# Two heads at a time in a recurrence, weights by halves, and a hold on small products in a planned three-layer kernel

## The chip, the cores and the metric

The kernel runs on one core of a Trainium2 chip. The metric is the device time of one execution in microseconds. Its engines are TensorE (PE, its weight loads PEld), VectorE (DVE), ScalarE (ACT), GpSimd (POOL) and SyncE (SP), whose queue issues the DMAs.

## What is computed

Input `x` is 256 tokens of width 2048. Three layers follow, each with a projection in, a mixer, a projection out and a residual. The first layer joins a sparse attention (8 heads) with an RWKV recurrence (16 heads of 64); the second is a differential attention (A), the third a gated linear attention with 4 heads (B). What matters here, cut to the core:

```python
def compress(kv, pos, w1, w2):                      # first layer, keys and values in blocks of 32
    flat = blocks_of_32(kv + pos)                   # (15 blocks, 2 groups, 32 * 128)
    return silu(flat @ w1) @ w2                     # w1: 4096 x 128

def step(state, inp):                               # RWKV, 16 heads, 256 steps
    r_t, w_t, k_t, v_t, a_t, b_t = inp
    sa = einsum('bhij,bhj->bhi', state, a_t)
    state = state * w_t[:, :, None, :] + sa[..., None] * b_t[:, :, None, :] + v_t[..., None] * k_t[:, :, None, :]
    return state, einsum('bhij,bhj->bhi', state, r_t)

def step(state, xs):                                # layer B, 4 heads, 4 chunks of 64 tokens
    qi, ki, vi, ti = xs
    state = exp(ti)[..., None] * state + einsum('bchk,bchv->bhkv', ki, vi)
    return state, einsum('bchk,bhkv->bchv', qi, state)
```

## The kernel before

**Who makes the order.** The program's instructions are first recorded as `Op`s. `Plan.schedule` (L279) then gives each engine a fixed order: it keeps a heap of ready operations for each engine and takes the one that can start first by estimated costs and due times, with program order as the tie break. `Plan.run` (L377) adds `SWITCH` (170 ns) to an estimate when TensorE goes from one tile size to another; `part` (L120) is that size in quarters of rows and columns, (4, 4) being the whole array. Operations on TensorE are due `MARGIN` (700 ns) later than their data, or 1500 ns behind a DMA. Since all instructions are issued on one line, every row of the profile says L277, and one goes by tile names. A tile can start only when its tag has a buffer, in program order within the tag.

**The bulk.** `gemm` streams 2048x512 weight groups: ScalarE makes the high part `wh_*`, VectorE the low part `wl_*`, and TensorE runs three products for each (`acc_*`, fp32r, 256 to 512 columns). All else is put between these products.

**The recurrence.** `rwkv_group` (L795) treats four heads at a time (g = 0 to 3), tokens in four chunks c of 64. `pA` holds products of a chunk with itself, which VectorE masks into `AB`. GpSimd inverts a triangular block of it (`blocks`), and the result comes back by way of DRAM as `M1` and `X`; `pT`, `pY` and `pX` complete the inverse, `pV` makes `M2` (the profile drops the numbers: both are `M`). Then comes the loop over c (from L976): `pU` = M1 times M2, copied into `AVt`; `pS`, the state for the next chunk, into `M2`; and `yp`, the output, from `AB` and, behind the first chunk, from `RT` and `M2`. Every product is for one head: 64 columns, and the output on the half of the array that belongs to the chunk (c even or odd). `yp` is one PSUM tile for the whole loop; two PSUM buffers serve this stream. `bn_stats` (L1007) then reads `yp`.

**Compression.** `compress` (L1137) is a generator, advanced after each weight tile of the third group's `rk` and `v`. For keys, then values, it loads `w1` in four parts of 512 KB and multiplies 8 slices of each into `ph`, 32 rows of the output at a time.

**Layer B's scores.** `gla_scores` (L1570) makes, for each head, decayed keys `d` (profile: `kd`), `q1`, `q2` (`q`) and `k2` (`k`), whose second half GpSimd copies (L1596). For each half j of the key dimension, six products of 64x64 go into `pB` and then one whole-array product of `k2` and `q2`.

## Time and profile before

| | us |
|---|---|
| median of 3 runs | 1483.45 (1483.18 to 1488.77) |
| the profiled execution | 1483.21 |
| its span, first to last instruction | 1481.4 |
| TensorE busy | 1454.8 (98%) |
| VectorE busy | 967.3 (65%) |
| ScalarE busy | 768.4 (52%) |
| GpSimd busy | 316.4 (21%) |

A product in fp32 stands in the trace as two MATMUL records, one in fp32r as one. TensorE overlaps its records, so a record's own duration is longer than the distance to the next start; distances between starts are what to read. The view "order of time" merges neighbours of one kind and gives the start of the first, the time to the end of the last, and how many.

### The profile page before, as it was taken

Reading aid. Unit: us, or ns where it says so; the run is one execution under the profiler, and the core shown is the slowest. Engines: PE = TensorE matmul, PEld = TensorE weight load, DVE = VectorE, ACT = ScalarE, POOL = GpSimd, SP = SyncE. Lnnn points to the kernel's source line nnn. Section 1 sums busy time; section 2 is a strip of 40 time slices with the busy share of each in tenths; the row PEclk is TensorE's granted clock in tenths of the full one; section 3 lists DMA queues with packets and bytes.
Section 4 is the critical chain, followed back from the end, with each engine's and each line's share of the span. In section 5 each row is a group of like instructions: output and inputs, shape, how many; then the busy total and the mean of one; then the engine's idle time right before and its main releaser. Section 6 shows DMA issues by size and latency. Waiting matters only on the chain.

```text
span 1481.4 us, 24543 instructions
## 1 busy us (share of the span) xinstructions
PE 1454.8 (98%) x9437; PEld 1278.9 (86%) x9437; DVE 967.3 (65%) x1678; ACT 768.4 (52%) x1269; POOL 316.4 (21%) x402
## 2 busy tenths in 40 slices
PE   8999999999999999999999999999999998999998
PEld 8988889989999988788888888788888897988887
DVE  5876575575857754876767676656765567565554
ACT  6542345344545544757575757554544473455532
POOL 0258846615600000030404050100100001000000
PEclk9999999999999999999999999999999999999999
DMA  9545434636524567665556566556665553655564
GB/s 334 182 131 198 160 97 139 194 104 183 156 82 148 165 218 228 212 190 174 182 171 185 167 180 215 174 186 197 205 208 186 173 172 110 222 174 185 185 213 128
DMA packets 91957, 263.42 MB, mean 178 GB/s; under 512 B 19960, under 2 KB 26512, under 8 KB 91840
## 3 DMA queue, kind: packets, MB, share of 16 engines
q1 hardware_dynamic: 91840, 261.86, 56.6%
q8 instruction: 74, 1.21, 0.3%
q14 instruction: 43, 0.35, 0.1%
HBM read 253.92 MB, written 7.90 MB: 177 GB/s over the span
## 4 chain that ended last, share of the span: by engine, by line
PE 90%; DVE 6%; issue 1%; ACT 1%; DMA 1%; POOL 1%; SPq 0%; DVEq 0%; ACTq 0%
PE acc_Bo L277 6%; PE acc_Aq L277 6%; PE acc_Ao L277 6%; PE acc_o L277 6%; PE acc_Ak L277 6%; PE acc_Av L277 6%; PE acc_rk L277 6%; PE acc_Bg L277 6%; PE acc_Ag L277 5%; PE acc_Bv L277 5%; PE acc_zb L277 3%; PE acc_Bq L277 3%; PE acc_q L277 3%; PE acc_Bk L277 3%; PE acc_v L277 3%; PE acc_za L277 2%
## 5 line engine op out<-in xcount | busy, mean ns | idle before, releaser
L277 PE MATMUL acc_rk<-xp,wh_rk 128*128 128x256 f32 x512 | 96.7, 289 | 1.3 <-ACT wh_rk L277 1.3
L277 PE MATMUL acc_Bo<-mBp,wh_Bo 128*128 128x512 f32 x256 | 89.7, 396 | 0.0
L277 POOL TENSOR_TENSOR bt<-blocks 32x30 f32<-32x30 f32 (+14 forms) x120 | 87.5, 729 | 9.0
L277 PE MATMUL acc_Ao<-mAp,wh_Ao 128*128 128x512 f32 x256 | 89.3, 395 | 0.0
L277 PE MATMUL acc_Bv<-wh_Bv,xBp 128*128 128x412 f32 (+1 forms) x320 | 88.3, 355 | 0.0
L277 PE MATMUL acc_Aq<-wh_Aq,xAp 128*128 128x512 f32 x256 | 86.0, 407 | 0.7 <-ACT xAp L277 0.7
L277 PEld LDWEIGHTS acc_rk<-xp,wh_rk 128*128 128x128 f32 x512 | 80.6, 193 | 4.9 <-issue 2.6
L277 POOL TENSOR_TENSOR blocks<-blocks,bt 32x30 f32<-32x30 f32 (+14 forms) x120 | 80.8, 673 | 9.3
L277 PE MATMUL acc_Ag<-wh_Ag,xAp 128*128 128x512 f32 x256 | 81.6, 395 | 0.0
L277 PE MATMUL acc_Ak<-wh_Ak,xAp 128*128 128x512 f32 x256 | 80.8, 392 | 0.0
L277 PE MATMUL acc_Av<-wh_Av,xAp 128*128 128x512 f32 x256 | 80.8, 392 | 0.0
L277 PE MATMUL acc_Bg<-wh_Bg,xBp 128*128 128x512 f32 x256 | 80.5, 393 | 0.0
L277 PE MATMUL acc_o<-wh_o,mp 128*128 128x512 f32 x256 | 79.8, 392 | 0.0
L277 PE MATMUL acc_rk<-xp,wl_rk 128*128 128x256 f32 x256 | 72.9, 286 | 0.5 <-DVE wl_rk L277 0.5
L277 PE MATMUL acc_Bo<-mBp,wl_Bo 128*128 128x256 f32 x256 | 71.1, 280 | 0.0
L277 PE MATMUL acc_Ao<-mAp,wl_Ao 128*128 128x256 f32 x256 | 70.9, 279 | 0.0
L277 DVE TENSOR_TENSOR wl_o<-wr_o,wh_o 128x1024 fp32r<-128x1024 f32 x32 | 39.2, 1225 | 38.2 <-ACT wh_o L277 38.0
L277 DVE TENSOR_TENSOR wl_Bo<-wr_Bo,wh_Bo 128x1024 fp32r<-128x1024 f32 x32 | 39.2, 1224 | 36.0 <-ACT wh_Bo L277 36.0
L277 DVE TENSOR_TENSOR wl_Bg<-wr_Bg,wh_Bg 128x1024 fp32r<-128x1024 f32 x32 | 39.2, 1225 | 33.9 <-ACT wh_Bg L277 33.9
L277 ACT ACTIVATE wh_Bo<-wr_Bo 128x1024 fp32r<-128x1024 f32 x32 | 34.0, 1062 | 51.8 <-PE acc_Bo L277 48.5
L277 PEld LDWEIGHTS acc_Bv<-wh_Bv,xBp 128*128 128x128 f32 x320 | 60.1, 190 | 0.9
L277 DVE TENSOR_TENSOR wl_rk<-wr_rk,wh_rk 128x1024 fp32r<-128x1024 f32 (+1 forms) x33 | 41.5, 1260 | 29.0 <-ACT wh_rk L277 29.0
(731 smaller groups left out, 4426.4 us busy)
## 6 DMA issues: line engine op xcount, KB each, us to landing
wr_o<-w SPq DMA_DIRECT2D x32, 512.0 KB, 3.6
wr_Aq<-w SPq DMA_DIRECT2D x32, 512.0 KB, 3.7
wr_Ak<-w SPq DMA_DIRECT2D x32, 512.0 KB, 3.7
wr_Av<-w SPq DMA_DIRECT2D x32, 512.0 KB, 3.9
wr_Ag<-w SPq DMA_DIRECT2D x32, 512.0 KB, 3.6
wr_Ao<-w SPq DMA_DIRECT2D x32, 512.0 KB, 3.8
wr_Bg<-w SPq DMA_DIRECT2D x32, 512.0 KB, 4.3
wr_Bo<-w SPq DMA_DIRECT2D x32, 512.0 KB, 3.9
```

The source lines that it names most:

```text
L277: op.issued = getattr(getattr(self.nc, op.eng), op.method)(*op.args, **op.kw)
```

## The change

The loop of the recurrence takes two heads in one product: the stationary and the moving operand each hold two heads side by side, the output is 128x128, and only the two diagonal 64x64 blocks are read. For that the layouts of `AB`, `M1` and `X` are turned (chunks outside, heads inside), `RT` is a full-height tile with zeros where it holds nothing (a 1-buffer tag of its own), `M2` has a zeroed half for the first chunk, and `yp` is one PSUM tile for each chunk, copied by ScalarE into an SBUF tile `ys`, which replaces `y`. VectorE masks `pA` in two instructions instead of one, and adds the state in two.

`compress` loads `w1` in two halves of two DMAs into a tag with one buffer, and multiplies the 16 slices of a half in reverse order. In `gla_scores` VectorE copies `k2` in place of GpSimd, and the whole-array products come behind all twelve small ones of the head. The planner adds `HOLD`: a product on a part of the array enters the heap 800 ns after its data are due, but while the last product was on a part of the array, held ones that are due may be taken at once. `pc4` has 3 buffers in place of 4, and the DMA scratch is 512 in place of 1024.

```diff
@@ Plan @@
+    HOLD = 800
@@ schedule @@
+        held = set()
+        partial = lambda op: op.eng == "tensor" and op.part[:2] != (4, 4)
+
+        def push(op):
+            time = ready[op]
+            if partial(op):
+                held.add(op)
+                time += self.HOLD
+            heapq.heappush(later[op.eng], (time, op.key, op))
+
         def candidate(eng):
             free, ahead, behind = self.free[eng], now[eng], later[eng]
+            if eng == "tensor" and self.part and self.part[:2] != (4, 4):
+                near = [op for op in held if ready[op] <= free]
+                near = [op for op in near for time, tag in [buffer_time(op)] if tag is None and time <= free]
+                if near:
+                    op = min(near, key=lambda op: op.key)
+                    return free, op.key, op
...
@@ Kernel @@
-    BUFS = {"t1": 6, "t2": 10, "t4": 5, "tiny": 24, "rtiny": 12, "rt4": 4, "rt2": 2, "rt1": 2, "rt8": 1}
+    BUFS = {"t1": 6, "t2": 10, "t4": 5, "tiny": 24, "rtiny": 12, "rt4": 4, "rt4z": 1, "rt1": 2, "rt8": 1}
@@ rwkv_group @@
-        RT = self.sb(f"RT{g}", [128, 2, 4, 64], "rt2")
-        for i in range(2):
-            for o in range(2):
-                S.activation(RT[hf(o), :, i:4:2, :].rearrange("p c j t -> p j c t"), AV[hf(i), :, 1 - o:4:2, 2, :], AF.Copy)
+        RT = self.sb(f"RT{g}", [128, 4, 4, 64], "rt4z")
+        for o in range(2):
+            G.memset(RT[hf(1 - o), 1 - o:4:2], 0.0)
+            for i in range(2):
+                S.activation(RT[hf(o), 1 - o:4:2, i:4:2, :].rearrange("p c j t -> p j c t"), AV[hf(i), :, 1 - o:4:2, 2, :], AF.Copy)
...
-        AB = (self.work if g % 2 else self.big).tile([128, 4, 4, 2, 64], F32, name=f"AB{g}", tag="ml")
+        at = lambda c: c % 2 * 2 + c // 2
+        of = lambda c1: slice(2 * c1, 2 * c1 + 2)
+        AB = (self.work if g % 2 else self.big).tile([128, 2, 4, 4, 64], F32, name=f"AB{g}", tag="ml")
...
             for i in range(2):
-                V.tensor_tensor(AB[:, 2 * j + i].rearrange("p c k t -> p c (k t)"), ps[i],
-                                cst[:, None, C_SI:C_SI + 128].to_broadcast([128, 4, 128]), op=OP.mult)
+                for k in range(2):
+                    V.tensor_tensor(AB[:, k, :, 2 * j + i], ps[i][:, :, 64 * k:64 * k + 64],
+                                    cst[:, None, C_SI + 64 * k:C_SI + 64 * k + 64].to_broadcast([128, 4, 64]), op=OP.mult)
...
+        G.memset(M2[hf(1), 0], 0.0)
...
-        yp = self.ps(f"yp{g}", U3)
+        ys = self.sb(f"ys{g}", U3, "t2")
+        pair = lambda x, j: x[:, 2 * j:2 * j + 2].rearrange("p h x -> p (h x)")
+        own2 = lambda p: [(i, p[hf(i), :, hf(i)]) for i in range(2)]
         for c in range(4):
             c1, c2 = c % 2, c // 2
             own, oth = hf(c1), hf(1 - c1)
-            rows = slice(0, 128) if c else own
-            pu = self.ps(f"pU{g}{c}", (128, 4, 64))
-            for h in range(4):
-                mm(pu[own, h], M1[rows, h, c], M2[rows, c, h], start=(h == 0), stop=True, skip_group_check=True)
-            S.activation(AVt[own, c], pu[own], AF.Copy)
+            pu = self.ps(f"pU{g}{c}", (128, 2, 128))
+            for j in range(2):
+                mm(pu[:, j], pair(M1[:, at(c)], j), pair(M2[:, c], j), start=(j == 0), stop=True, skip_group_check=True)
+            for i, p in own2(pu):
+                S.activation(AVt[own, c, i:4:2], p, AF.Copy)
             if c < 3:
-                pS = self.ps(f"pS{g}{c}", (128, 4, 64))
-                for h in range(4):
-                    mm(pS[own, h], BKt[:, c, h], AVt[:, c, h], start=(h == 0), stop=True, skip_group_check=True)
-                pc = PC[own, c].rearrange("p j i -> p (j i)")[:, :, None].to_broadcast([64, 4, 64])
+                pS = self.ps(f"pS{g}{c}", (128, 2, 128))
+                for j in range(2):
+                    mm(pS[:, j], pair(BKt[:, c], j), pair(AVt[:, c], j), start=(j == 0), stop=True, skip_group_check=True)
                 Sn = M2[own, c + 1]
...
-            for h in range(4):
-                o = yp[own, c2 * 4 + h]
-                mm(o, AB[:, h, c, 1], AVt[:, c, h], start=(c2 == 0 and h == 0), stop=not c, skip_group_check=True)
+            yp = self.ps(f"yp{g}{c}", (128, 2, 128))
+            for j in range(2):
+                mm(yp[:, j], pair(AB[:, 1, at(c)], j), pair(AVt[:, c], j), start=(j == 0), stop=not c, skip_group_check=True)
             if c:
-                for h in range(4):
-                    mm(yp[own, c2 * 4 + h], RT[oth, c2, h], M2[oth, c, h], start=False, stop=True, skip_group_check=True)
+                for j in range(2):
+                    mm(yp[:, j], pair(RT[:, c], j), pair(M2[:, c], j), start=False, stop=True, skip_group_check=True)
+            for i, p in own2(yp):
+                S.activation(ys[own, 4 * c2 + i:4 * c2 + 4:2], p, AF.Copy)
...
-            V.bn_stats(st[:, u], yp[:, u])
+            V.bn_stats(st[:, u], ys[:, u])
@@ compress @@
-            for part in range(4):
-                w1 = self.sb(f"w1_{kind}{part}", [128, 8, 128], "t4")
-                nc.sync.dma_start(w1, a["cw1"][kind, part])
-                for l in range(8):
-                    ll, o = part * 8 + l, l % 4 * 32
-                    mm(ph[o:o + 32], wins[kind][:, ll], w1[:, l], start=(ll < 4), stop=(ll >= 28), skip_group_check=True)
-                if part < 3:
+            for half in range(2):
+                w1 = self.sb(f"w1_{kind}{half}", [128, 2, 8, 128], "w1")
+                for part in range(2):
+                    nc.sync.dma_start(w1[:, part], a["cw1"][kind, 2 * half + part])
+
+                for l in reversed(range(16)):
+                    ll, o = half * 16 + l, l % 4 * 32
+                    mm(ph[o:o + 32], wins[kind][:, ll], w1[:, l // 8, l % 8], start=(half == 0 and l >= 12), stop=(half == 1 and l < 4), skip_group_check=True)
+                if half == 0:
                     yield
@@ nsa_group @@
-        pc4 = [self.sb(f"pc{g}{t}", [128, 4, 4, 32], "pc4", bufs=4) for t in range(2)]
+        pc4 = [self.sb(f"pc{g}{t}", [128, 4, 4, 32], "pc4", bufs=3) for t in range(2)]
@@ gla_scores @@
-            G.tensor_copy(k2[:, :, 1], d[:, :, 1])
+            V.tensor_copy(k2[:, :, 1], d[:, :, 1])

             p = self.ps(f"pB{h}", (128, 3, 128))
+            st = lambda j: dict(stop=(j == 1), skip_group_check=True)
             for j in range(2):
-                st = dict(stop=(j == 1), skip_group_check=True)
                 for i, c in enumerate((0, 2)):
-                    mm(p[0:64, 2 * i, 0:64], d[:, j, c], q[:, j, c], start=(i == 0 and j == 0), **st)
-                    mm(p[0:64, 2 * i, 64:128], d[:, j, c], q1[:, j, i], start=False, **st)
-                    mm(p[64:128, 2 * i, 64:128], d[:, j, c + 1], q[:, j, c + 1], start=(i == 0 and j == 0), **st)
+                    mm(p[0:64, 2 * i, 0:64], d[:, j, c], q[:, j, c], start=(i == 0 and j == 0), **st(j))
+                    mm(p[64:128, 2 * i, 64:128], d[:, j, c + 1], q[:, j, c + 1], start=(i == 0 and j == 0), **st(j))
+                    mm(p[0:64, 2 * i, 64:128], d[:, j, c], q1[:, j, i], start=False, **st(j))
+            for j in range(2):
                 f2 = lambda x: x[:, j].rearrange("p c t -> p (c t)")
-                mm(p[:, 1], f2(k2), f2(q2), start=False, **st)
+                mm(p[:, 1], f2(k2), f2(q2), start=False, **st(j))
@@ kernel @@
-    nc = bacc.Bacc("TRN2", target_bir_lowering=False, num_devices=1, dynamic_dma_scratch_size=1024)
+    nc = bacc.Bacc("TRN2", target_bir_lowering=False, num_devices=1, dynamic_dma_scratch_size=512)
```

## Rows read from the trace of the kernel before

**Rows 1.** The page: span, and each engine's busy us (share) and instructions.

```profile
span 1481.4 us, 24543 instructions
...
PE 1454.8 (98%) x9437; PEld 1278.9 (86%) x9437; DVE 967.3 (65%) x1678; ACT 768.4 (52%) x1269; POOL 316.4 (21%) x402
```

**Rows 2.** Order of time, TensorE: start us, us, operation, records; group 0's loop.

```profile
164.56 0.28 PE L277 MATMUL acc_rk<-xp,wl_rk 128*128 128x256 f32 x1
164.77 0.68 PE L277 MATMUL pS<-AVt,BKt 128*64 128x64 f32 x8
165.29 0.63 PE L277 MATMUL yp<-AVt,AB 128*64 128x64 f32 x8
165.85 0.50 PE L277 MATMUL acc_rk<-xp,wh_rk 128*128 128x256 f32 x2
166.19 0.28 PE L277 MATMUL acc_rk<-xp,wl_rk 128*128 128x256 f32 x1
166.31 0.40 PE L277 MATMUL acc_rk<-xp,wh_rk 128*128 128x256 f32 x2
...
166.66 0.40 PE L277 MATMUL acc_rk<-xp,wh_rk 128*128 128x256 f32 x2
166.99 0.68 PE L277 MATMUL pU<-M,M 128*64 128x64 f32 x8
167.60 0.39 PE L277 MATMUL acc_rk<-xp,wl_rk 128*128 128x256 f32 x1
167.82 0.40 PE L277 MATMUL acc_rk<-xp,wh_rk 128*128 128x256 f32 x2
```

**Rows 3.** Order of time, TensorE: the last visit of group 3's loop.

```profile
430.07 0.68 PE L277 MATMUL yp<-AVt,AB 128*64 128x64 f32 x8
430.68 0.67 PE L277 MATMUL yp<-M,RT 64*64 64x64 f32 x8
431.28 0.39 PE L277 MATMUL acc_q<-xp,wh_q 128*128 128x256 f32 x1
```

**Rows 4.** Order of time, TensorE: whole-array fp32 products inside a gemm.

```profile
692.73 0.62 PE L277 MATMUL acc_Aq<-wh_Aq,xAp 128*128 128x512 f32 x2
693.19 0.83 PE L277 MATMUL poA<-vA,PTA 128*128 128x128 f32 x6
693.77 0.48 PE L277 MATMUL acc_Aq<-wl_Aq,xAp 128*128 128x512 f32 x1
694.09 0.63 PE L277 MATMUL acc_Aq<-wh_Aq,xAp 128*128 128x512 f32 x2
```

**Rows 5.** Order of time, GpSimd and TensorE: the wait in layer B's scores.

```profile
1229.70 3.55 POOL L277 COPY k<-kd 128x128 f32<-128x128 f32 x1 [133.76 <-DVE kd L277]
...
1233.31 0.80 PE L277 MATMUL pB<-q,k 128*128 128x128 f32 x2 [2.94 <-POOL k L277]
```

**Rows 6.** Stretches: length, each engine's busy us, then PEclk, DMA share, GB/s.

```profile
104.00:114.00 10.00, 6.71 (x36) 5.27 (x35) 9.38 (x13) 1.28 (x2) 9.43 (x13) 0.83 0.46 156
...
1225.00:1230.00 5.00, 4.10 (x29) 3.66 (x28) 5.00 (x10) 2.63 (x5) 0.30 (x1) 1.00 0.50 158
1230.00:1240.00 10.00, 7.06 (x48) 5.91 (x45) 6.61 (x16) 2.53 (x4) 3.55 (x2) 0.66 0.29 84
```

**Rows 7.** The tile yp: its first products, ns min/median/max, first and last start.

```profile
L277 PE MATMUL yp<-AVt,AB x128: 222/222/270, 165.3 to 430.5; 128*64 128x64 f32 x128
```

**Rows 8.** Groups of instructions by form, ScalarE: the copies out of pU.

```profile
L277 ACT ACTIVATE AVt<-pU 64x256 f32<-64x256 f32 x16 | 6.0, 376 | 25.0 <-PE pU L277 24.9
```

**Rows 9.** Order of time, TensorE: compression's last block, and the first pT.

```profile
154.11 0.65 PE L277 MATMUL ph<-w,win 128*32 128x128 f32 x16 [1.04 <-DMA w<-cw]
...
157.70 0.89 PE L277 MATMUL pT<-X,AB 32*32 32x32 f32 x32 [1.80 <-DMA X<-dx]
```

**Rows 10.** Order of time, TensorE: group 0's pV, in two pieces.

```profile
74.10 0.56 PE L277 MATMUL pV<-AVt,AB 64*64 64x64 f32 x12
...
74.91 0.80 PE L277 MATMUL pV<-AVt,AB 64*64 64x64 f32 x20
```

## What the change is predicted to do

> **What bounds the kernel now.** The page comes first: TensorE is busy for 98% of the span, the next engine, VectorE, for 65%, ScalarE for 52% [rows 1]. The end is therefore set by what stands in TensorE's queue, and by what the queue holds up. A busy share hides two things, so the second view is TensorE's order of time, read from start to start and not by the durations, which overlap.
>
> The first thing is the cost of a visit. I call a visit a stretch of products on a part of the array (fewer than 65 rows or columns) between two whole-array products. Around the first lone visits of group 0's recurrence [rows 2] an `acc_rk` product of 256 columns starts every 0.12 us (166.19 to 166.31). From 164.56 to 166.19 stand three of them and 16 records of `pS` and `yp`: 1.63 - 0.36 = 1.27 us for the 16. From 166.66 to 167.82 stand three and 8 records of `pU`: 1.16 - 0.36 = 0.80 for 8. The difference gives 0.059 us a record, and what is left is 0.33 us for each visit, whatever it holds. A change of tile size inside a visit costs less: `yp` with 128 rows and then 64 rows takes 431.28 - 430.07 = 1.21 us for 16 records [rows 3], where 16 of one size took 165.85 - 164.77 = 1.08 [rows 2]. That is 0.13 us a change. A whole-array fp32 product pays neither: from 692.73 to 694.09 stand three `acc_Aq` of 0.23 and six records of `poA`, 1.36 - 0.69 = 0.67 us, 0.112 a record of 128 columns and nothing for coming and going [rows 4]. I counted 75 visits in the order of time, 66 up to 432 us and 9 around 1230 to 1251.
>
> The second thing is waits that end in something other than TensorE. The largest that the change touches is at 1230: the first `pB` of 128x128 waits 2.94 us for `k`, one GpSimd copy that took 3.55 us [rows 5]. Behind it the granted clock falls: over 1230 to 1240 it is 0.66, so TensorE was at 1.2 GHz for two thirds of it, while it is 1.00 in the stretch before [rows 6].
>
> **The change part by part.** All sums go against the profiled execution: 1483.2 us, of which the span is 1481.4; it lies 0.2 under the median of the three runs.
>
> *Recurrence by two heads.* Each product stands as two records (`yp<-AVt,AB`: 64 products by the code, 128 records [rows 7]). A group has 56 small products now, 16 `pU`, 12 `pS`, 16 and 12 into `yp`, 112 records at 0.059, 6.6 us. After: 28 whole products, 56 records at 0.112, 6.3 us. Four groups: 1.3 us less. Half of each new product is computed for nothing, but the other half rides along. The loop is on TensorE in 7 visits a group; of the 28, 24 hold nothing else and go (24 x 0.33 = 7.9 us); four are shared with `ph` or `pA` and stay, with 7 inner changes less; 12 inner changes in `yp` go too (19 x 0.13 = 2.5). **11.7 us** in all. Bounds: 8 if the new products pay for alternating with fp32r products, which [rows 4] speak against; 12.5 if what they leave joins up.
>
> What is added is off TensorE. ScalarE: 32 copies in place of 16 out of `pU` (0.376 each for 64x256 [rows 8], the halves less), 32 more out of `yp`; under 18 us spread over some 260, on an engine half idle. VectorE: four more mask products a group and three more for the state, at the page's mean of 967.3/1678 = 0.58 us, 16 us at most, less what `bn_stats` saves by reading SBUF. GpSimd: 12 memsets at 316.4/402 = 0.79 us, 9.4 us in all [rows 1]. Each step of the loop gets one more copy into its latency. `acc` products stand on both sides of the visits in [rows 2, 3], and they cover it; if that cover were gone, 16 steps times 0.376 would be 6 us. `yp` no longer holds one of the two PSUM buffers through the loop, which loosens `pU` and `pS`. The single `RT` buffer makes the next group's copy wait for this group's last `yp`; the next `RT` is read only a whole stage later. I take 0 for all of these, 0 to 6.
>
> *Compression by halves.* Eight blocks of 16 records stand in six visits of their own, the last at 154.11 [rows 9], and in two shared ones. Afterwards there are four blocks of 32. Two visits and two inner changes go: 0.66 + 0.26 = **0.9 us**. On SP each half but the first waits for the products of the half before (one buffer), and the weight tiles issued behind wait with it. Four tiles of weights lie ahead, and `kc` and `vc4` are wanted only by the attention, so I take 0; the other end is two waits like the 1.04 us that `ph` shows today [rows 9].
>
> *Layer B's scores.* Nine visits (each head's two halves j apart, one of them torn) become four: 5 x 0.33 = **1.7 us**. The `k2` copy goes to VectorE, ahead of products that now come last in the head: the 2.94 us wait goes. So does the slow stretch, if nothing else leaves TensorE idle there: 10 x (1 - 0.66) = 3.4 us of clock, less the part that ran during the wait, 3.0. VectorE is busy for 5.00 of 5.00 us just before [rows 6], so some of this turns into waits for it: I give back 1.0. **4.9 us**, bounds 0 and 5.9.
>
> *The hold.* A partial product that is ready waits 800 ns in the plan unless TensorE is already on a part of the array. Where a group of them is torn (`pV`, 12 records at 74.10 and 20 at 74.91 [rows 10]; four such places) it is joined: three of four, **1.0 us**, 0 to 1.3. The hold also works as spare time for partial products whose data come late: `ph` waits 1.04 us for its weights and `pT` 1.80 for `X` [rows 9]; 0.8 off each, **1.3 us**, 0 to 1.6. What is queued behind a held product is the rest of its group's chain (`pT`, `pY`, `pX`, then the loop); TensorE meanwhile takes `acc` products. Where there are none it idles, a rival below.
>
> Sum: 11.7 + 0.9 + 1.7 + 4.9 + 1.0 + 1.3 = 21.5 us. 1483.2 - 21.5 = 1461.7, with the 0.2 to the median **1462.0 us**.
>
> A rule that speaks against the change. The rows: a record of 64 columns on 128x64 takes 0.059, a whole one of 128 columns 0.112 [rows 2, 4], so two heads cost the same either way; `pV`, whose neighbours write different halves, takes less, 20 records in 0.80 us [rows 10]. The Trainium skill (TensorEngine Tiling (Array Packing), Theoretical Speedup) promises up to 2x where a dimension is 64 or less, because tiles run at once. By that rule the change throws away a gain; the trace does not show it for the loop, whose four products of a step all write the same half.
>
> **The rivals.**
> (a) *VectorE takes the place of GpSimd at 1230.* Its full 5.00 us [rows 6] speak for it; that it falls to 6.61 of 10 behind the wait speaks against. The 4.9 us stay: 1467.
> (b) *The joining does not happen*: compression, scores and torn groups keep their visits, since the order is made from planned times. 0.9 + 1.7 + 1.0 + 1.3 stay: 1467.
> (c) *The new order also loses the hole at 104 to 114*, where TensorE is busy for 6.71 of 10 us at a clock of 0.83 [rows 6]: 3.3 + 1.7 = 5.0 more: 1457.
> (d) *New holes.* Every start moves, and an order fixed ahead waits wherever the plan is early. Two like the one at 1230, each with its slow stretch, cost 2 x (2.9 + 3.0): 1474.
> (e) *Slower: the hold idles TensorE.* Some 38 visits are left. If at each no `acc` product is at hand, 38 x 0.8 = 30 us are lost against 21.5 won: 1492. It decides from 27 of the 38 on. The hole at 104 shows that TensorE can run dry; the `acc` products around nearly every visit speak against it.
> (f) *Packing*: if the old loop really ran two records at once, at half of 0.059, the new one costs 3 us a group more and the gain is 9.5: 1474.
>
> **How the numbers follow.** Chances: the forecast (1457 to 1467 with its own bounds) 0.50, (a) 0.15, (b) 0.10, (c) 0.08, (d) 0.10, (e) 0.05, (f) 0.02. The range from 1452 to 1474 leaves out (e), half of (d) and the tail of (c). A measurement of this kernel can tell about 0.5%, 7.4 us, from no change, so faster means under 1476. All but (e) and half of (d) are: 0.90; same 0.05, slower 0.05.
>
> **What would show it.** In the profile after: the `pU`, `pS` and `yp` records are 128x128, start 0.11 us apart, and the `acc` products next to them keep their spacing. Visits fall from 75 to about 38. `ph` comes in four blocks, `pB` in one visit a head, with no GpSimd copy and a clock of 1.00 around 1210 to 1230. TensorE's busy time falls by nearly as much as the span. I am wrong if `acc` products start late next to the new ones, if the span falls by much less than TensorE's own work (then the waits view names who is late: VectorE `kd`, `M` or DMA `w`), or if TensorE idles ahead of held products.

## The result, and the profile after

| | us |
|---|---|
| before, median of 4 runs | 1484.65 (1483.18 to 1488.77) |
| after, median of 4 runs | 1467.17 (1464.47 to 1467.73) |
| ratio, with its 95% interval | 0.9873 [0.9859, 0.9887] |
| the profiled execution after, and its span | 1467.73, 1465.6 |

The changed kernel is 17.5 us faster by the medians, 18.9 (16.8 to 20.9) by the ratio, and 15.5 by the two profiled executions. The forecast was 21.5 us and a time of 1462.0; 1467.2 lies inside the range.

The page after, span and busy times; it answers [rows 1]:

```profile
span 1465.6 us, 24194 instructions
...
PE 1439.7 (98%) x9213; PEld 1273.2 (87%) x9213; DVE 971.2 (66%) x1710; ACT 778.6 (53%) x1317; POOL 316.4 (22%) x410
```

TensorE's busy time fell by 15.1 us, the span by 15.8; VectorE gained 3.9 us and ScalarE 10.2, beside other work.

Order of time of TensorE after, one visit of the loop; it answers [rows 2, 3, 7]:

```profile
190.24 0.28 PE L279 MATMUL acc_kk<-xp,wl_kk 128*128 128x256 f32 x1
190.36 0.28 PE L279 MATMUL acc_kk<-xp,wh_kk 128*128 128x256 f32 x1
190.48 0.61 PE L279 MATMUL yp<-AVt,AB 128*128 128x128 f32 x4
190.93 0.61 PE L279 MATMUL yp<-M,RT 128*128 128x128 f32 x4
191.29 0.36 PE L279 MATMUL acc_kk<-xp,wh_kk 128*128 128x256 f32 x1
191.50 0.28 PE L279 MATMUL acc_kk<-xp,wl_kk 128*128 128x256 f32 x1
```

From 190.48 to 191.50 stand eight whole records and one `acc_kk` of 0.12: (1.02 - 0.12) / 8 = 0.1125 us a record, and nothing on top. Counted over the trace, visits fell from 75 to 34 and changes of tile size from 175 to 76.

Stretches after (length, then busy us of PE, PEld, DVE, ACT and POOL, PEclk, DMA share, GB/s); the first, fourth and fifth answer [rows 6]:

```profile
104.00:114.00 10.00, 7.97 (x68) 7.76 (x66) 9.96 (x16) 4.34 (x7) 9.77 (x8) 1.00 0.35 124
155.00:162.00 7.00, 5.08 (x59) 4.68 (x48) 2.35 (x2) 1.06 (x1) 6.24 (x11) 1.00 0.54 141
162.00:170.00 8.00, 7.45 (x111) 6.90 (x113) 5.14 (x9) 2.56 (x5) 5.32 (x10) 0.57 0.64 239
1225.00:1230.00 5.00, 4.15 (x22) 3.76 (x23) 4.49 (x15) 1.79 (x3) 0.00 (x0) 1.00 0.38 123
1230.00:1240.00 10.00, 9.15 (x85) 8.26 (x84) 9.56 (x22) 4.35 (x9) 0.00 (x0) 1.00 0.46 128
```

Two of the same stretches in the trace of before, which were not among its rows:

```profile
155.00:162.00 7.00, 5.20 (x102) 4.37 (x102) 0.36 (x1) 1.94 (x5) 6.15 (x12) 1.00 0.80 291
162.00:170.00 8.00, 8.00 (x116) 6.97 (x112) 3.71 (x7) 3.50 (x6) 7.21 (x11) 1.00 0.21 69
```

At 1230 the clock is 1.00 where it was 0.66 [rows 6]. In this execution 162 to 170 fell to 0.57 instead, where before it was 1.00. TensorE's waits after, longest first (us in total, times, longest):

```profile
PE pnb L279 <- DVE sq L279: 3.8, 2, 2.4
PE pT L279 <- DMA X<-dx: 2.5, 1, 2.5
...
PE pB L279 <- DVE k L279: 0.9, 1, 0.9
...
PE pB L279 <- DVE kd L279: 0.7, 1, 0.7
```

The same view of before:

```profile
PE pnb L277 <- DVE sq L277: 3.2, 2, 2.8
PE pB L277 <- POOL k L277: 2.9, 1, 2.9
PE pT L277 <- DMA X<-dx: 2.3, 2, 1.8
```

The 2.9 us behind GpSimd are gone [rows 5]. `pT` now waits once for 2.5 us, up to 162.5, and TensorE runs slowly from there. One execution does not show that the wait brings the slow stretch; the last section has this place in four more executions.

To put the whole span of a profiled execution into terms I use three for every kernel below, a ledger. *Waits* is the sum of the waits view. *Low clock* is the time at 1.2 GHz by the granted clock, of which half is lost. The *rest*, span - waits - (low clock)/2, is TensorE's own work with its comings and goings. (A wait that lies in such a stretch is in both, so the rest is somewhat low where the low clock is large.) The last column is not of the profiled execution alone: the mean granted clock is on record for every execution, and span x (1 - clock), what the low clock costs, is averaged over all of them.

| kernel | median, us | ratio to before | span | visits | changes | waits | low clock | rest | clock cost, all |
|---|---|---|---|---|---|---|---|---|---|
| before | 1484.65 | 1 | 1481.4 | 75 | 175 | 22.3 | 13.7 | 1452.3 | 9.1 |
| after | 1467.17 | 0.9873 [0.9859, 0.9887] | 1465.6 | 34 | 76 | 21.3 | 13.7 | 1437.5 | 5.9 |
| e1 loop alone | 1481.41 | 0.9968 [0.9956, 0.9980] | 1483.0 | 48 | 106 | 25.8 | 34.1 | 1440.1 | 12.6 |
| e2 scores alone | 1479.26 | 0.9948 [0.9931, 0.9964] | 1478.7 | 70 | 165 | 21.7 | 13.7 | 1450.2 | 5.2 |
| e3 hold alone | 1480.75 | 0.9966 [0.9953, 0.9979] | 1479.9 | 54 | 148 | 24.3 | 23.9 | 1443.6 | 9.9 |
| e4 halves alone | 1485.80 | 0.9997 [0.9986, 1.0007] | 1484.2 | 75 | 167 | 25.3 | 20.5 | 1448.6 | 9.1 |
| e5 after, `pT` due later | 1465.88 | 0.9864 [0.9845, 0.9883] | 1465.3 | 33 | 75 | 22.1 | 13.7 | 1436.4 | 5.1 |
| e6 after without halves | 1471.37 | 0.9897 [0.9879, 0.9914] | 1471.1 | 31 | 76 | 27.8 | 18.2 | 1434.2 | 8.1 |
| e7 e5, `pnb` due later too | 1465.68 | 0.9863 [0.9844, 0.9881] | 1463.8 | 31 | 73 | 18.8 | 18.0 | 1436.0 | 7.3 |
| e8 copy alone | 1481.34 | 0.9970 [0.9957, 0.9982] | 1477.9 | 75 | 175 | 19.3 | 14.9 | 1451.2 | 6.2 |
| e9 visits added | 1512.65 | 1.0189 [1.0169, 1.0208] | 1508.1 | 106 | 237 | 23.3 | 17.1 | 1476.2 | 9.8 |
| e10 the same, whole array | 1499.88 | 1.0094 [1.0078, 1.0111] | 1495.5 | 75 | 175 | 24.2 | 10.7 | 1465.9 | 9.0 |
| e11 after without hold | 1466.31 | 0.9868 [0.9854, 0.9882] | 1463.3 | 43 | 89 | 19.8 | 6.8 | 1440.1 | 3.7 |
| e12 after, hold of 0 ns | 1474.05 | 0.9919 [0.9903, 0.9934] | 1470.5 | 38 | 83 | 23.2 | 20.5 | 1437.0 | 10.8 |

(Ratios go against the runs of before that were made beside each kernel; its median there was 1485.45 to 1486.25.) First reading: between the two profiled executions the rest fell by 14.8 us, waits by 1.0, the low clock by nothing. Most of the gain is work that TensorE no longer does. Over all executions the clock has a share too: it costs 9.1 us before (56 executions made beside these kernels) and 5.9 after (four: 7.3, 7.3, 7.3 and 1.5, each good to 0.7, as the clock is recorded to 0.001). So of the 18.9 us some 3 are clock and some 16 work and waits, the 14.8 + 1.0 of the ledger.

### The profile page after: what moved, and what is told of

The parts are those of the page before. It is cut to its first block, busy times and chain, and to the rows that moved or that the text cites. A ratio compares the mean times of both kernels' runs of the same rounds, so it can differ in the third digit from the quotient of the medians.

```text
span 1465.6 us, 24194 instructions
## 1 busy us (share of the span) xinstructions
PE 1439.7 (98%) x9213; PEld 1273.2 (87%) x9213; DVE 971.2 (66%) x1710; ACT 778.6 (53%) x1317; POOL 316.4 (22%) x410
## 4 chain that ended last, share of the span: by engine, by line
PE 78%; DVE 5%; ACT 2%; issue 1%; DMA 1%; SPq 0%; DVEq 0%; ACTq 0%
PE acc_Bo L279 6%; PE acc_Ao L279 6%; PE acc_o L279 6%; PE acc_Aq L279 6%; PE acc_Ak L279 6%; PE acc_Av L279 6%; PE acc_Bg L279 6%; PE acc_Ag L279 5%; PE acc_Bv L279 4%; PE acc_zb L279 3%; PE acc_Bq L279 3%; PE acc_Bk L279 3%; PE acc_q L279 3%; PE acc_rk L279 2%; PE acc_za L279 2%
## 5 line engine op out<-in xcount | busy, mean ns | idle before, releaser
L279 POOL TENSOR_TENSOR blocks<-blocks,bt 32x30 f32<-32x30 f32 (+14 forms) x120 | 94.8, 790 | 9.1
L279 POOL TENSOR_TENSOR bt<-blocks 32x30 f32<-32x30 f32 (+14 forms) x120 | 77.1, 643 | 9.1
```

The source lines that it names most:

```text
L279: op.issued = getattr(getattr(self.nc, op.eng), op.method)(*op.args, **op.kw)
```

## Experiments

My theory was that the gain is the price of visits, and that a late transfer in the first layer keeps back the remainder. The rivals put the gain, or the lack of it, on waits alone, on the order of the plan, or on one part of the change.

**One part at a time: the loop.** The kernel before with the hunks of the recurrence, and the buffers that they need (`pc4` and the smaller scratch among them):

```diff
-    BUFS = {"t1": 6, "t2": 10, "t4": 5, "tiny": 24, "rtiny": 12, "rt4": 4, "rt2": 2, "rt1": 2, "rt8": 1}
+    BUFS = {"t1": 6, "t2": 10, "t4": 5, "tiny": 24, "rtiny": 12, "rt4": 4, "rt4z": 1, "rt1": 2, "rt8": 1}
...
-                mm(pu[own, h], M1[rows, h, c], M2[rows, c, h], start=(h == 0), stop=True, skip_group_check=True)
+                mm(pu[:, j], pair(M1[:, at(c)], j), pair(M2[:, c], j), start=(j == 0), stop=True, skip_group_check=True)
```

> The kernel before with the recurrence by two heads alone (and the two buffer sizes that make room for it). If the gain is TensorE's own work: 24 lone visits and 19 inner changes of tile size go, 24 x 0.33 + 19 x 0.13 + 1.3 = 11.7 us, so about 1472; visits fall from 75 to about 51, no wait grows by over 1 us. If alternating whole fp32 products with fp32r products has a price of its own, the acc products next to them start late and at most 8 us are won (1476). If it is the hold that wins in the whole change, this one alone stays within 3 us of the kernel before.

Measured: 0.9968, 4.7 us less, and not the 1472 expected. The rest fell by 12.2 us, for 11.7 forecast, and all of it was given back within the same execution: waits +3.5, low clock +20.4, of which half is lost. Over its ten executions the clock costs 12.6 us, 3.5 more than before; with the 3.5 of waits that makes up the 7.0 that are missing. From the waits of this kernel:

```profile
PE pT L277 <- DMA X<-dx: 4.3, 2, 2.2
```

and two of its stretches:

```profile
155.00:170.00 15.00, 12.04 (x158) 10.18 (x159) 3.07 (x2) 4.52 (x8) 13.38 (x22) 0.66 0.55 190
295.00:312.00 17.00, 14.72 (x166) 12.86 (x165) 12.16 (x23) 8.57 (x18) 2.80 (x9) 0.80 0.65 203
```

Two waits of `pT` for `X` (2.06 at 157, 2.23 at 299), with clocks of 0.66 and 0.80 around them; before waited 2.3 for `X` in all, and stayed at 1.00 over 162 to 170. What makes `X` late here was not tried by itself. (The profiled execution was the slowest of this kernel's, 3.4 us above its median.)

**The scores.** The kernel before with the hunk of `gla_scores`:

```diff
-            G.tensor_copy(k2[:, :, 1], d[:, :, 1])
+            V.tensor_copy(k2[:, :, 1], d[:, :, 1])
...
+            for j in range(2):
...
-                mm(p[:, 1], f2(k2), f2(q2), start=False, **st)
+                mm(p[:, 1], f2(k2), f2(q2), start=False, **st(j))
```

> The kernel before with layer B's new order of scores and the copy of k2 on VectorE alone. By the prediction: 5 visits (1.7 us), the 2.94 us wait for GpSimd and 3.0 us of slow clock go, 1.0 comes back as waits for VectorE: 6.6 us less, about 1477. In the whole change this stage gave 6.9 us (the gain at the first acc_Bg less that at the last acc_Bk). Rival: VectorE, full before the stage, takes the place of GpSimd, and the slow stretch stays: 1.7 us, 1482.

Measured: 0.9948, 7.7 us less; 5 visits and 10 changes fewer, and no wait for GpSimd. The forecast for this part was 6.6.

**The copy alone.** Only the first two lines of that diff.

> The kernel before with the k2 copy on VectorE alone, the order of the scores as it was. If the copy is the cause, the 2.94 us wait and the slow stretch of 6.83 us behind it go: 4.5 to 6 us less, 1479; the order of the scores then is worth the 1.7 us of the visits. Rival: without the new order the first whole product still waits (for VectorE, which now makes the copy too, ahead of it), and most of the wait stays: 1 to 2 us less.

Measured: 0.9970, 4.5 us (2.7 to 6.4), with visits and changes exactly as before. The stretch that [rows 6] shows at a clock of 0.66, in this kernel:

```profile
1230.00:1240.00 10.00, 8.60 (x79) 6.78 (x77) 9.83 (x24) 4.10 (x6) 0.00 (x0) 1.00 0.50 153
```

So the one GpSimd copy was the cause of the wait and of the slow stretch at this place, 4.9 us by the forecast. In this one execution the low clock came elsewhere (14.9 in all), but over all executions it costs 6.2 us against the 9.3 of those of before made beside it, 3.1 less for the 3.0 of the forecast. The other 3.2 of e2 would go with the order of the scores, whose five visits were put at 1.7; the intervals of e2 and e8 overlap, so the times do not settle this share. The stage itself is nearer: from the first `acc_Bv` to the first `acc_Bg` it takes 111.2 us before, 106.2 in e8, 104.9 in e2 and 104.2 after, so 5.0 for the copy and 1.3 for the order. (In e9 and e10 below, with the copy on GpSimd and less low clock behind it, it takes 110.0.)

**The hold.** The kernel before with the hunks of the planner:

```diff
+    HOLD = 800
...
+            if partial(op):
+                held.add(op)
+                time += self.HOLD
```

> The kernel before with the planner's hold of 800 ns alone. If it joins what is torn: some 10 to 20 of the 75 visits go, 3 to 7 us, 1477 to 1480. Rival: the hold leaves TensorE without work, 0.8 us at a good part of the visits, and delays the inverse: slower by 5 us or more, with waits ahead of partial products. Second rival: it makes the wait for X at the first pT longer, since pu and pa of group 0 start later; then the wait that the whole change shows there (2.47 us) is the hold's doing.

Measured: 0.9966, 5.0 us less, where the forecast gave this part 2.3. It joins far more than three torn groups: 21 visits fewer, 21 x 0.33 = 6.9 us. Only 27 changes of size go with them, where 21 visits alone have 42, so 15 more stand inside the visits that are left: 6.9 - 15 x 0.13 = 4.9. As spare time for late data it does nothing: `ph` waits 2.6 us in two places, where it waited 1.0, and `pT` 2.5 where it waited 2.3. The waits of this kernel:

```profile
PE ph L279 <- DMA w<-cw: 2.6, 2, 1.5
PE pT L279 <- DMA X<-dx: 2.5, 2, 1.6
```

The longest wait for `X` is no longer than before (1.8), so nothing speaks for the second rival.

**The halves.** The kernel before with the hunk of `compress`, 3 buffers for `pc4` and the smaller scratch:

```diff
-            for part in range(4):
-                w1 = self.sb(f"w1_{kind}{part}", [128, 8, 128], "t4")
+            for half in range(2):
+                w1 = self.sb(f"w1_{kind}{half}", [128, 2, 8, 128], "w1")
```

> The kernel before with the compression weights by halves alone (and the buffer sizes). The theory: 1 MB of w1 goes into the DMA queue ahead of the small transfers dy and dx of group 0, so dy lands 4 us later than it does today (2.35 us from issue to landing), SP waits for it, X comes late, and TensorE waits 2.5 us or more at the first pT, with a stretch at 1.2 GHz behind it: 0.9 us of work won, 2 to 5 lost, 1483 to 1488. Rival: the wait in the whole change comes from the hold and the late start of group 0; then this kernel gains its 0.9 us and the wait at pT stays at 1.8 us, no slow stretch, 1482.

Measured: 0.9997 [0.9986, 1.0007], nothing. The forecast of 0.9 us lies within the interval. The queue of the theory came, its wait did not: `dy` goes out at 148.72 behind two `w`, `M<-dy` 7.0 us later at 155.72, and the first `pT` still waits less than the 1.80 of before:

```profile
162.38 0.79 PE L277 MATMUL pT<-X,AB 32*32 32x32 f32 x20 [1.34 <-DMA X<-dx]
```

So a late `dy` alone need not lengthen that wait. The rival's "no slow stretch" did not come either: the clock is 0.89 over 155 to 170.

Alone, the four parts bring 4.7 + 7.7 + 5.0 + 0.4 = 17.8 us, the whole 18.9. That the sum fits so well is chance, as the next ones show.

**The whole without the halves.** The reverse of the last diff on the changed kernel (`pc4` and the scratch stay as changed).

> The changed kernel with the compression weights by quarters as before. If the halves' 1 MB ahead of dy is what makes X late past the plan, dy lands within 3 us of its issue again, the wait at the first pT falls under 1 us and the slow stretch there goes, against two to four visits more (0.7 to 1.3 us): 2 to 4 us less than the changed kernel. Rival, by the halves alone, which showed a wait of 1.34 there: the plan reckons with the queue, the wait stays near 2 us, and this kernel is within 1.5 us of the changed one.

Measured: 0.9897, against 0.9873 some 3.6 us slower (the intervals, up to 0.9887 and from 0.9879, overlap a little), which no theory had. It has 3 visits fewer and a rest 3.3 us lower; it waits 6.5 us more (`ph` 2.83 for `w` up to 160, `pT` 3.67 for `X` up to 305.6). What speaks for the order with halves is where its late data fall, and not its work.

**The wait of `pT`.** After the change SyncE's queue reads, from 146 to 159 us:

```profile
146.50 1.84 SPq L279 DMA_DIRECT2D w<-cw  x2
148.51 0.34 SPq L279 DMA_DIRECT2D dy<-blocks  x1
...
154.77 3.23 SPq L279 DMA_DIRECT2D M<-dy  x4
...
158.53 0.92 SPq L279 DMA_DIRECT2D X<-dx  x2
```

and before:

```profile
144.78 0.34 SPq L277 DMA_DIRECT2D dy<-blocks  x1
...
147.14 1.33 SPq L277 DMA_DIRECT2D M<-dy  x3
...
152.04 0.99 SPq L277 DMA_DIRECT2D X<-dx  x2
```

`dy` now goes out behind 1 MB of compression weights, and `M<-dy` can be issued 6.3 us behind it (2.4 before); `X` goes out 6.5 us later. I took this for the missing 4 to 6 us, and moved the due time of `pT` in the plan:

```diff
-            return d.end + self.DMA_MARGIN[op.eng == "tensor"]
+            late = 3500 if op.eng == "tensor" and any(x.tensor.name[0] == "X" for x, _ in op.uses) else 0
+            return d.end + self.DMA_MARGIN[op.eng == "tensor"] + late
```

> The changed kernel with one edit in the plan: products that read X (only pT does) are due 3.5 us later behind the DMA. Theory: the 4 to 6 us that the prediction has too much went into the wait at the first pT (2.47 us) and into the stretch at 1.2 GHz behind it (6.83 us, so 3.4 lost); with pT placed behind the landing both go: 4 to 6 us less than the changed kernel, 1461 to 1463, and no slow stretch near 160. Rival: the slow stretch comes of the light products there (pT and pY on a quarter of the array) and not of the wait; then only the wait goes, 2 us or less.

Measured: 0.9864 [0.9845, 0.9883], no different from the whole. The wait for `X` is gone; `ph` now waits 1.76 for `w` and `pU` 1.96 for `M`, and waits and low clock total what they did (22.1 and 13.7). That theory fell. With `pnb` moved too:

```diff
+        if op.method == "transpose" and op.args[0].tensor.name.startswith("pnb"):
+            margin += 3000
```

> As the margin for X, and the transposes pnb are due 3 us later than the plan has them: they wait 1.42 and 2.38 us for VectorE's sq in the changed kernel, with a slow stretch of 3.41 us behind the second. If waits that the plan does not foresee are all that is left to win here, another 3 to 5 us go: 1457 to 1460. Rival: TensorE has no other product at hand there (VectorE is busy for 9.58 of 10 us from 110 to 120, and low parts of the weights come from it too), so the wait only moves to acc_kvc: no difference to the margin for X alone.

Measured: 0.9863 [0.9844, 0.9881], again the same. The `pnb` waits are gone, `pA` waits 3.0 and `pU` 2.9, and the clock falls at another place, with TensorE busy all through:

```profile
121.00:132.00 11.00, 11.00 (x52) 8.86 (x51) 3.47 (x8) 1.54 (x2) 9.82 (x16) 0.53 0.36 105
```

**The price of a visit by itself.** Products that nothing uses, behind each of the 32 weight tiles of `Ao`, in the kernel before; four of 64 columns on 128x64, or two of 128 on the whole array:

```diff
+            if group[:2] == "Ao":
+                w, o = hi.bitcast(F32), self.ps(f"dm{group}{k0}", (128, 2, 128))
+                for j in range(4):
+                    mm(o[0:64, 0, 0:64], w[:, 0, 64 * j:64 * j + 64], w[:, 1, 0:64], start=True, stop=True, skip_group_check=True)
```

```diff
+                for j in range(2):
+                    mm(o[:, 0], w[:, 0, 128 * j:128 * j + 128], w[:, 1, 0:128], start=True, stop=True, skip_group_check=True)
```

> The kernel before, with work added that nothing uses: behind each of the 32 weight tiles of Ao, four fp32 products of 64 columns on 128x64 (8 records). Nothing is left out. Theory (a visit costs 0.33 us on top of its records): 32 x (0.33 + 8 x 0.059) = 25.7 us more, 1511. Rival (the cost of coming and going is hidden behind the neighbours in Ao, as it would be if it came from waiting for data in the recurrence): 32 x 8 x 0.059 = 15.1 us more, 1500.

> The kernel before, with work added that nothing uses: behind each of the 32 weight tiles of Ao, two whole-array fp32 products of 128 columns (4 records), the same number of columns as in the run with four small ones. Nothing is left out. Theory (whole products pay no coming and going): 32 x 4 x 0.112 = 14.3 us more, 1499, so 11 us under the run with small ones. Rival (every group of fp32 products among fp32r ones pays the 0.33): 25 us more, 1509, as much as the small ones.

Measured: +28 us and +14 us by the ratios. Nearer is the stretch from the first `acc_Ao` to the first `acc_Bq`, by the rows of the tiles (duration min/median/max, first and last start). Before:

```profile
L277 PE MATMUL acc_Bq<-xBp,wh_Bq x128: 387/395/500, 1086.2 to 1132.0; 128*128 128x512 f32 x128
L277 PE MATMUL acc_Ao<-mAp,wh_Ao x256: 387/392/478, 995.4 to 1085.7; 128*128 128x512 f32 x128
```

with the small products:

```profile
L277 PE MATMUL acc_Bq<-xBp,wh_Bq x128: 390/392/497, 1114.5 to 1160.1; 128*128 128x512 f32 x128
L277 PE MATMUL acc_Ao<-mAp,wh_Ao x256: 387/398/501, 997.9 to 1113.5; 128*128 128x512 f32 x128
```

and with the whole ones:

```profile
L277 PE MATMUL acc_Bq<-xBp,wh_Bq x128: 390/392/496, 1102.1 to 1147.6; 128*128 128x512 f32 x128
L277 PE MATMUL acc_Ao<-mAp,wh_Ao x256: 387/395/497, 997.0 to 1101.4; 128*128 128x512 f32 x128
```

90.8 us before, 116.6 with the small products (+25.8, expected 25.7), 105.1 with the whole ones (+14.3, expected 14.3). The 32 groups of small products stand in 31 visits (the first three groups in one, the fourth in two). With 256 x 0.059 = 15.1 us for their records a visit costs (25.8 - 15.1) / 31 = 0.345 us, for 0.33 forecast, and whole products cost their records alone. The rows of one visit show where it sits:

```profile
1030.14 0.40 PE L277 MATMUL acc_Ao<-mAp,wh_Ao 128*128 128x512 f32 x1
1030.38 0.28 PE L277 MATMUL acc_Ao<-mAp,wl_Ao 128*128 128x256 f32 x1
1030.59 0.68 PE L277 MATMUL dmAo<-wh_Ao 128*64 128x64 f32 x8
1031.20 0.50 PE L277 MATMUL acc_Ao<-mAp,wh_Ao 128*128 128x512 f32 x1
1031.53 0.28 PE L277 MATMUL acc_Ao<-mAp,wl_Ao 128*128 128x256 f32 x1
```

The first small one starts 0.21 us behind a `wl` that takes 0.12 elsewhere; the eight take 0.61 and not 0.47; the `wh` behind them takes 0.33 and not 0.24: 0.09 + 0.14 + 0.09 = 0.32. Nothing in this gemm waits for data of the recurrence, so the price is that of the tile sizes. The Trainium skill (TensorEngine Tiling (Array Packing), Key Properties) says that a change of tiling mode drains TensorE; these rows agree, and give the price that the page leaves open.

**The whole without the hold, and with a hold of nothing.** The changed kernel without the planner's hunks; and with

```diff
-    HOLD = 800
+    HOLD = 0
```

> The changed kernel without the hold of the planner; all else as changed. Theory (the hold joins visits inside the whole as it did alone): visits rise from 34 to between 44 and 54, 3 to 7 us at 0.33 us each, 1470 to 1474. Rival (what it joins is given back in waits, as the joining and the waits of the first layer were): within 2 us of the changed kernel, 1465 to 1469.

> The changed kernel with the hold's 800 ns set to 0: products on a part of the array that are ready are still taken together once one has run, but none waits. Theory (the gain of the hold is in taking together, the 800 ns add spare time only): within 2 us of the changed kernel, 1465 to 1469. Rival (without the 800 ns there is nothing ready to take together, and the plan has less spare time before late data): as without the hold, 1470 to 1474.

Measured: without the hold 0.9868 [0.9854, 0.9882], no different from the whole, so for the first kernel the rival was right; with a hold of nothing 0.9919 [0.9903, 0.9934], 6.8 us slower than the whole. The second kernel has the time that its rival gave, but not the reason: it has 38 visits, between the other two (34 and 43), and a rest as low as the whole's. The `X` of a later group is late, by TensorE's order of time:

```profile
303.36 0.86 PE L279 MATMUL pT<-X,AB 32*32 32x32 f32 x20 [4.05 <-DMA X<-dx]
```

and the clock falls there:

```profile
295.00:315.00 20.00, 15.95 (x171) 15.29 (x171) 11.89 (x22) 8.80 (x19) 3.86 (x9) 0.74 0.63 198
```

Without the hold the nine visits more cost 9 x 0.33 = 3.0 us (the rest is 2.6 higher), and 1.5 us of waits and 3.4 of clock are won back.

## Why the prediction was right, and where it was wrong

**TensorE's own work: right.** The terms of work were 11.7 (loop) + 0.9 (halves) + 1.7 (score visits) + 1.0 (joins) = 15.3 us; the rest fell by 14.8. The new records take 0.1125 us against 0.112 from [rows 4], their neighbours start in time, and a visit measured alone costs 0.345 us for 0.33. About 38 visits were forecast, 34 came (the prediction's own terms, 24 + 2 + 5 + 3, leave 41 of the 75 and not 38); the loop alone lowers the rest by 12.2 for 11.7. That 14.8 meets 15.3 so nearly is in part luck: at the prediction's prices the 41 visits, 17 inner changes and 1.3 us of records that went make 13.5 + 2.2 + 1.3 = 17.0, and the ledger is good to some 3.5 us (last section). Rival (f) (packing) is out by the records themselves: e9 and e10 do the same columns, and the small ones cost 0.81 us a group against 0.45, 0.47 of it their records. The doubling of the Trainium skill (TensorEngine Tiling (Array Packing), Theoretical Speedup) does not show for products that write one half of the array. Where neighbours write different halves the trace does show half the price: the 8 records that the second piece of `pV` has more take 0.80 - 0.56 = 0.24 us [rows 10], 0.03 each for 0.059, and their starts come in pairs. A loop that alternates halves was not tried.

**Inside that sum the hold was mis-sized.** Its joins were put at three of four torn groups, 1.0 us; alone it takes 21 visits away, 5.0 us measured. In the whole it is worth nothing that can be measured (e11). Rival (b), that joining does not happen, is out; rival (e), that TensorE idles ahead of held products, too: the longest waits after end in VectorE's `sq` and in `X`, which are late data.

**The scores: right.** 6.6 forecast, 7.7 alone, and in the whole layer B's stage is shorter by 7.0 (from the first `acc_Bv`, 8.7 us earlier than before, to the first `acc_Bg`, 15.7 earlier). The copy is the cause of most of it (e8). The 1.0 given back for waits on VectorE did not come: `pB` waits 0.85 for `k` and 0.75 for `kd`, where 0.8 and 0.9 for these two stood before beside the 2.94. Rival (a) is out.

**Waits and clock: the step that failed.** "The 2.94 us wait goes. So does the slow stretch" and "0.8 off each" for `ph` and `pT` made 4.9 + 1.3 = 6.2 us (twice 0.8 would be 1.6; the prediction does not say where the 1.3 comes from). What it says of 1230 happened, and in the profiled executions the total still moved by only 1.0 us of waits and none of low clock. The shortfall stands ahead of layer B's scores: up to the first `acc_Bv`, 21.5 - 6.6 = 14.9 us were forecast and 8.7 came. There, in these two executions, `pT` went from 1.80 to 2.47, with the clock at 0.57 for 8 us, 8 x 0.43 = 3.4 us lost, and `pnb` from one long wait of 2.81 to two of 1.42 and 2.38. `ph` did improve, from 1.04 [rows 9] to 0.31. Over all executions the clock term came, some 3 us (9.1 to 5.9) for 3.0. What failed is the waits: 2.94 + 1.3 - 1.0 = 3.2 us forecast, 1.0 measured in the profiled executions; and over all executions work and waits together give some 16 for 15.3 + 3.2 = 18.5. The prediction looked at what the halves delay on SyncE and named only tiles of weights; `dy`, and with it `M` and `X`, stand there too. That queue alone did not lengthen the wait (e4). And the late `X` is not a bill that could be avoided: with its due time moved (e5) or `pnb`'s as well (e7), others wait instead. This is rival (d) in kind. That its price for one hole, 21.5 - 5.9 = 15.6 us, meets the 15.5 of the profiled executions is chance: the hole at 160 is 0.67 us of wait and 3.4 of clock, 4.1, and executions of the old order wait as long there, or run slowly there too (last section). New waits should have been part of the forecast, not a case beside it: in the new orders tried one by one (e1, e3, e5, e6, e7, e12), `pT`, `ph`, `pU` or `pA` waits longer somewhere than before.

**Rival (c)** did not come: at 104 to 114 TensorE is busy for 7.97 us where it was 6.71, but `pnb` still waits 2.38 us and the clock still falls behind it, at 114.

What is open: why one plan lands on few waits and another on many. The four that differ least in work (after, e5, e7, e12: rests of 1436.0 to 1437.5) have medians from 1465.7 to 1474.1, and in the traces waits and half of the low clock make 28.2, 29.0, 27.8 and 33.5 us. I have no rule that tells it ahead. Open as well is what makes `X` late in e1, e6 and e12.

## What to carry to other kernels

Count TensorE's visits to other tile sizes and price them by starts: here 0.33 us each in the recurrence and 0.345 alone in a gemm, and doing two heads in one whole product costs the same columns without the visits. Book such work as TensorE's own, which goes for good, but reckon with waits and low clock that a new order brings (the loop alone: 12.2 us of work gone, 4.7 us won). Book a wait removed from a planned order only as far as nothing else is late in the same stage; price it at zero to its full size. Do not explain a kernel by one wait of one trace; run the same order more than once. What one part of a change is worth alone or left out (the hold 5.0 and 0, the halves 0.4 and 3.6) is not a property of the part where each edit makes a new order, so try parts in the company in which they will stay.

## What the hardware showed that I had not expected

The same order of instructions meets different waits. Up to the first `acc_Ao` at 995 us the kernels e2, e8, e9 and e10 issue what the kernel before does, in the same order on every engine. In the five executions (before first) it starts at 995.4, 999.0, 997.3, 997.9 and 997.0 us, and the one wait of `pnb` before 111 us took 2.81, 2.79, 2.79, 4.77 and 2.80:

```profile
110.72 1.12 PE L277 MATMUL pnb<-cst,sq 128*128 128x128 f32 x4 [4.77 <-DVE sq L277]
```

A difference of 2 us in one wait between two traces is therefore no finding by itself, and the ledger of a single execution is good to some 3.5 us; that is more than lies between the gain by the profiled executions (15.5) and by the medians (17.5). (By the recorded clocks the profiled execution of before lost 1.7 us less than the mean of its kernel, that of after 1.5 more.)

It holds for the first `pT` and the clock behind it too. The wait took 1.80, 2.52, 1.98, 1.55 and 1.38 us, and the granted clock over 160 to 168 was 1.00, 1.00, 0.84, 0.79 and 1.00. The longest of these waits, in e2, with its clock, and then the lowest clock, in e9:

```profile
160.03 0.90 PE L277 MATMUL pT<-X,AB 32*32 32x32 f32 x32 [2.52 <-DMA X<-dx]
160.00:168.00 8.00, 7.97 (x160) 6.94 (x161) 1.41 (x2) 4.01 (x8) 7.22 (x11) 1.00 0.44 154
160.00:168.00 8.00, 8.00 (x143) 7.07 (x139) 1.57 (x1) 4.01 (x8) 7.22 (x11) 0.79 0.36 142
```

So a wait like the 2.47 after, and a slow stretch at this place, come and go in one and the same order, and the change need not have made either.

A GpSimd copy of 128x128 took 3.55 us as the first one, from 1229.70 to 1233.25 [rows 5], and 0.29, 0.29 and 0.66 for the next three (by the order of time on GpSimd before):

```profile
1236.00 0.29 POOL L277 COPY k<-kd 128x128 f32<-128x128 f32 x1 [2.74 <-PE pB L277]
1241.94 0.29 POOL L277 COPY k<-kd 128x128 f32<-128x128 f32 x1 [5.65 <-PE pB L277]
1246.53 0.66 POOL L277 COPY k<-kd 128x128 f32<-128x128 f32 x1 [4.30 <-PE pB L277]
```

The first one stands behind 134 us of idleness, but that is not what its length follows. It lies beside an unbroken run of VectorE's TENSOR_TENSOR, and VectorE then stops until 1236.43, as the last of the run and the next instruction show:

```profile
1232.43 0.68 DVE L277 TENSOR_TENSOR kd<-ge 128x512 f32<-128x512 f32 x1
1236.43 0.50 DVE L277 CAST ATB0h<-pB 64x128 fp32r<-64x128 f32 x2 [3.32 <-ACT ATB0h L277]
```

The run ends at 1233.11 and the copy 0.14 us behind it; the two copies of 0.29 fall into gaps of VectorE. In all six kernels with the copy on GpSimd the first one ends 0.14 to 0.15 us behind such a run: 3.55 to 3.56 us in five of them, and 5.09 in e3, where the run goes on for 4.94 us (and `pB` waits 4.47). Beside VectorE's CAST it took 0.29 (e3). So the copy was held up for as long as VectorE ran TENSOR_TENSOR; no run here moves those instructions to prove it.

The clock does not follow one wait alone: behind 2.52 us of `pT` in e2 it stayed at 1.00, behind 2.47 us after it fell to 0.57. Around the same wait of `pB`, 2.94 us for the copy, it was 0.66 over ten us before [rows 6], and 0.83 in e10:

```profile
1246.00:1256.00 10.00, 7.06 (x57) 6.01 (x56) 6.87 (x16) 2.53 (x4) 3.20 (x2) 0.83 0.24 79
```

And in e7 it fell to 0.53 around 121 to 132, where `pA` had waited 0.69 and 1.20 just ahead.
